# Weight sums of a block product by accumulating DMA, vector sums off GpSimd, prompt rows transposed in spare columns

## Chip, core and metric

The kernel runs on one NeuronCore of a Trainium2 chip, as one launch of one program. The metric is device time in microseconds (us). The engines go by the profile's names: PE (TensorE, with its weight loads as PEld), DVE (VectorE), ACT (ScalarE), POOL (GpSimd) and SP (SyncE, which mainly issues DMAs). Each works through its own instruction stream in order and waits on semaphores.

## What is computed

One layer for 128 prompt tokens and 512 sample tokens of width 1024: a modulated input `h`, a wide projection `h @ w_in`, a gated long convolution by FFT in one branch, windowed attention with 16 heads of 64 in the other, a merge, an output projection and a layer norm. Cut to what matters:

```python
h = x * (1 + scale) + shift
z = h @ w_in                                   # D_IN = 10240 columns
hy, g_h, qkv, g_a, m = split(z)
hy = short_conv(hy, conv_w, conv_b)            # 3 taps
v_h, x1, x0 = split(hy)
u = v_h * x1
y_h = (irfft(rfft(u, 2L) * rfft(filt, 2L))[:L] + u * d_bias) * x0
y_a = attention(q, k, v)                       # sample: 8 x 16 window + context keys; prompt: full
p_h = (y_h * silu(g_h)) @ w_bh
p_a = (y_a * silu(g_a)) @ w_ba
m_h, m_a = split(sigmoid(m))
out = (m_h * p_h + m_a * p_a) @ w_out
x_new = layer_norm(ALPHA * x + gate * out, ln_g, ln_b)
```

The prompt's keys and values are outputs too (`new_k`, `new_v`).

## The kernel before

Every large matmul is made of three passes over operands split in a high part (rounded to fp32r) and a low part (the rest): high x high, high x low, low x high. `split` (L100) makes them: ACT casts the high part (L101), and DVE or GpSimd subtracts it (L102). `hH` and `hL` are the split input, eight blocks of 128 channels by 640 tokens. Weights lie in DRAM as `wall[i]`, 128 x 1024 tiles, and are loaded into two `raw` buffers by SP.

The work has five stages. The prologue (0 to about 55 us) makes the modulated input. The convolution phase (55 to 366) projects the tiles of `hy` on PE and weaves in FFT products. `conv_tile` (L464) evacuates a projection on ACT and adds the outer taps with two instructions on DVE (L477). `product_in_blocks` (L458) multiplies by `x0` on GpSimd. Meanwhile `token_sums` (L685) makes on GpSimd the sums t1 to t4 of blocks of `h`, split, and stores them in DRAM (`tok_d`). The transition (366 to 403) reloads them as `t`. The attention phase (403 to 777) makes the other projections in 22 pairs of tiles and weaves attention into them; a tail (777 to 965) projects, merges and normalizes.

A pair is a 2 x 2 block product with seven block products instead of eight (`pair_tile`, L1067). Its two weight tiles give blocks a11, a12 (first tile) and a21, a22 (second tile). `prepared` (L1039) makes seven weight blocks `wb{tile}_{j}`: j = 0, 4, 5 are a11, a12, a22; s2 = a11 - a21 (j = 2), s1 = s2 - a22 (1) and s6 = a12 + s1 (6) are sums on DVE, s3 = a21 + a22 (3) is one on GpSimd (L1049). Each is split: the low parts of j = 0, 4, 5 are GpSimd's, the rest DVE's. Five `wb` buffers go round. `prepared` is advanced one step per product, so weight blocks come several products ahead, the next pair's first ones during the last products of the pair before.

A head `j` of attend (two heads of 64, L1012) is woven into two or three pairs, counted in half products. `tiled(i)` puts scores of two query blocks in four PSUM banks, does the value products of older blocks, and computes the softmax: a row maximum on DVE (L892), the exponential on ACT (L897), a scaling on GpSimd (L899; L952 for the prompt block `pp`). `turned(i)` transposes the softmax tiles of the two blocks before on PE (L915) into banks `pt` and copies them on ACT (L917) to `pts`. Four banks exist for this (`aux`). For the first block of a head it also transposes the prompt rows `pp` to a bank `ptp` (L1007), copied to `ptsp` (L1009). `pp` and the middle blocks' softmax tiles share one ring of five buffers, `p`; the outer blocks lie in `edge` buffers.

Outside the prologue, a recording layer decides where an instruction stands on its engine, from the order of the code and its own estimate of when inputs are there.

## Time and profile before

| | us |
|---|---|
| median of 3 runs | 969.93 (968.72 to 970.64) |
| the profiled execution's own time | 966.56 |
| its span, first to last instruction | 964.8 |
| mean granted TensorE clock | 0.972 of full |
| busy: PE / DVE / ACT / POOL | 892.5 / 666.8 / 441.2 / 346.2 |
| DMA | 148.76 MB |

In a group's row stand line, engine, operation, output <- inputs by names, shape, and xcount; then busy us and mean ns of one; then the engine's idle time just before such instructions and what ended it. A row of waits reads: who <- what it waited for, us in total, times, longest. A row of the timeline starts with its start in us and its length; a bracket holds the idle time before. A row of windows gives busy us of PE, PEld, DVE, ACT and POOL, the granted clock, the share of the DMA engines and GB/s. Rows of DMA issues end with the median time from issue to landing.

### The profile page before, as it was taken

Reading aid. Unit: us, or ns where it says so; the run is one execution under the profiler, and the core shown is the slowest. Engines: PE = TensorE matmul, PEld = TensorE weight load, DVE = VectorE, ACT = ScalarE, POOL = GpSimd, SP = SyncE. Lnnn points to the kernel's source line nnn. Section 1 sums busy time; section 2 is a strip of 40 time slices with the busy share of each in tenths; the row PEclk is TensorE's granted clock in tenths of the full one; section 3 lists DMA queues with packets and bytes.
Section 4 is the critical chain, followed back from the end, with each engine's and each line's share of the span. In section 5 each row is a group of like instructions: output and inputs, shape, how many; then the busy total and the mean of one; then the engine's idle time right before and its main releaser. Section 6 shows DMA issues by size and latency. Waiting matters only on the chain. (4 is left out here: it accounts for less than half of the span.)

```text
span 964.8 us, 17002 instructions
## 1 busy us (share of the span) xinstructions
PE 892.5 (93%) x6464; PEld 850.8 (88%) x6464; DVE 666.8 (69%) x1179; ACT 441.2 (46%) x950; POOL 346.2 (36%) x330
## 2 busy tenths in 40 slices
PE   8799999799999997798988989999898999999994
PEld 7699999799999996698988989888888889999883
DVE  4887766984794786577676857677676558577565
ACT  4276445444644524454555546555556532143200
POOL 0740115542210304584764666556746500000000
PEclk9999999899999998899999999999999999999997
DMA  8966675567564514743534252613433377535331
GB/s 333 365 182 140 139 175 133 149 162 175 136 133 126 138 55 175 277 149 98 166 97 150 75 165 93 193 59 113 138 109 107 107 251 270 208 137 201 120 106 66
DMA packets 61998, 148.76 MB, mean 154 GB/s; under 512 B 9531, under 2 KB 27195, under 8 KB 61916
## 3 DMA queue, kind: packets, MB, share of 16 engines
q1 hardware_dynamic: 49580, 116.90, 36.7%
q0 software_dynamic: 6720, 25.17, 11.9%
q10 hardware_dynamic: 5616, 5.61, 1.7%
q8 instruction: 51, 0.84, 0.3%
q14 instruction: 31, 0.25, 0.1%
HBM read 123.66 MB, written 23.99 MB: 153 GB/s over the span
## 5 line engine op out<-in xcount | busy, mean ns | idle before, releaser
L1080 PE MATMUL sp<-t,wb 128*128 128x320 f32 x1056 | 180.4, 323 | 22.6 <-POOL wb L102 11.4
L1080 PEld LDWEIGHTS sp<-t,wb 128*128 128x128 f32 x1056 | 164.6, 196 | 30.0 <-POOL wb L102 13.3
L1080 PE MATMUL sp<-hH,wb 128*128 128x320 f32 x528 | 128.1, 314 | 0.0
L102 POOL TENSOR_TENSOR wb<-raw,wb 128x512 fp32r<-128x512 f32 x66 | 89.5, 1360 | 87.9 <-ACT wb L101 79.6
L170 PE MATMUL mm<-hH,wh 128*128 128x320 f32 x416 | 100.5, 315 | 4.2 <-ACT hH L316 4.0
L170 PE MATMUL mm<-hH,wl 128*128 128x320 f32 x416 | 99.9, 312 | 0.4 <-DVE wl L102 0.4
L170 PE MATMUL mm<-hL,wh 128*128 128x320 f32 x416 | 99.7, 312 | 0.3 <-DVE hL L317 0.3
L1080 PEld LDWEIGHTS sp<-hH,wb 128*128 128x128 f32 x528 | 91.1, 189 | 3.3 <-issue 2.5
L150 POOL DMA_DIRECT2D wl<-wall x28 | 25.0, 891 | 164.1 <-ACT wl L149 142.7
L101 ACT ACTIVATE wb<-s 128x512 fp32r<-128x512 f32 x88 | 54.7, 627 | 62.7 <-DVE s L1049 40.0
L1080 PE MATMUL sp<-hL,wb 128*128 128x320 f32 x264 | 81.8, 310 | 0.0
L102 DVE TENSOR_TENSOR wb<-s,wb 128x512 fp32r<-128x512 f32 x88 | 71.1, 819 | 14.4 <-ACT wb L101 14.1
L170 PEld LDWEIGHTS mm<-hH,wh 128*128 128x128 f32 x416 | 70.8, 190 | 6.0 <-ACT hH L316 4.5
L170 PEld LDWEIGHTS mm<-hL,wh 128*128 128x128 f32 x416 | 71.1, 190 | 1.5 <-DVE hL L317 1.1
L170 PEld LDWEIGHTS mm<-hH,wl 128*128 128x128 f32 x416 | 71.1, 190 | 1.5 <-DVE wl L102 0.9
L1359 POOL TENSOR_TENSOR r<-r,bc 128x64 f32<-128x64 f32 x1 | 0.3, 320 | 182.2 <-ACT r L1358 182.2
L899 POOL TENSOR_SCALAR p<-p,sm 128x384 f32<-128x384 f32 x32 | 46.6, 1462 | 34.2 <-DVE sm L898 34.1
L101 ACT ACTIVATE wb<-raw 128x512 fp32r<-128x512 f32 x66 | 41.1, 623 | 34.7 <-DMA raw<-wall 24.6
L151 ACT ACTIVATE wh<-raw 128x1024 fp32r<-128x1024 f32 x28 | 29.7, 1059 | 52.7 <-PE mm L170 37.5
L1080 PEld LDWEIGHTS sp<-hL,wb 128*128 128x128 f32 x264 | 50.0, 189 | 0.0
L1049 DVE TENSOR_TENSOR s<-raw,raw 128x512 f32<-128x512 f32 x22 | 16.8, 762 | 43.3 <-DMA raw<-wall 42.4
L101 ACT ACTIVATE wh<-raw 128x1024 fp32r<-128x1024 f32 x21 | 22.1, 1059 | 52.3 <-PE mm L170 41.5
(356 smaller groups left out, 2291.5 us busy)
## 6 DMA issues: line engine op xcount, KB each, us to landing
raw<-wall SPq DMA_DIRECT2D x96, 512.0 KB, 3.7
wl<-wall POOLq DMA_DIRECT2D x28, 512.0 KB, 6.1
ada<-wada SPq DMA_DIRECT2D x16, 512.0 KB, 8.2
tm<-bias SPq DMA_DIRECT2D x16, 512.0 KB, 5.0
tok_d<-t POOLq DMA_DIRECT2D x16, 320.0 KB, 5.2
t<-tok_d SPq DMA_DIRECT2D x16, 320.0 KB, 5.6
gate<-wgate SPq DMA_DIRECT2D x8, 512.0 KB, 5.0
wo<-wall SPq DMA_DIRECT2D x8, 512.0 KB, 3.9
```

The costliest lines, as they stand in the source:

```text
L101: hi = nc.scalar.activation(dst_h, src, AF.Copy)
L102: return hi, (eng or nc.vector).tensor_tensor(dst_l, src, f(dst_h), op=ALU.subtract)
L150: nc.gpsimd.dma_start(wl, a["wall"][i], accum_op=ALU.add)
L151: nc.scalar.activation(wh, raw[:], AF.Copy)
L170: nc.tensor.matmul(ps[hf][:, :HALF], wt[k], x[:, hf * HALF : (hf + 1) * HALF], start=(i == 0 and k == 0), stop=(i == lead[2] and k == NK - ...
L899: nc.gpsimd.tensor_scalar_mul(pv, pv, sm[:, 2:3])
L1049: (nc.gpsimd if j in ON_POOL["sums"] else nc.vector).tensor_tensor(src[j], x, y, op=op)
L1080: nc.tensor.matmul(dst, wk, x(xi, k), start=j < 4 and k == 0 and i == 0, stop=k == 3 and i == 2, skip_group_check=True,)
L1359: nc.gpsimd.tensor_tensor(r[:, h], r[:, h], bc[:, 0, h], op=ALU.mult)
```

## The change

GpSimd is left with scalings, memsets, a last small sum and DMA issues. (1) Token sums and products with `x0` go to DVE, the high parts of the token sums to ACT, and the product in `gates_h` to DVE. (2) In `prepared` the second tile counts with its sign turned, so s2 = a11 + a21 and s3 = a21 + a22 need only additions of weights. s3 is made in place by a DMA from DRAM that adds onto a21 in the raw tile; s2 is loaded a second time from DRAM and gets a21 by such a DMA. Both are issued by GpSimd. s1 = s2 + a22 and s6 = a12 + s1 stay on DVE, and all seven low parts are DVE's. Where the second tile's result is used its sign is turned back by a scale or a constant. (3) All keys of the prompt are copied once on ACT before they are stored. (4) The prompt rows are transposed together with the third block (b = 2) of their head into columns 384 to 511 of its banks, and copied with it; the copies have 512 columns and four buffers.

```diff
     def product_in_blocks(y, x, u):
-        nc.gpsimd.tensor_tensor(y[:, :LP], x[:, :LP], u[:, :LP], op=ALU.mult)
+        nc.vector.tensor_tensor(y[:, :LP], x[:, :LP], u[:, :LP], op=ALU.mult)
...
-    def gate(th, p):
-        nc.vector.scalar_tensor_tensor(th, th, 1.0, p[:, :HALF], op0=ALU.add, op1=ALU.mult)
+    def gate(th, p, one=1.0):
+        nc.vector.scalar_tensor_tensor(th, th, one, p[:, :HALF], op0=ALU.add, op1=ALU.mult)
...
-        def step(dst, x, i, j, op):
+        def step(dst, i, j, op):
             for t in (hH, hL):
-                nc.gpsimd.tensor_tensor(dst, x, part(t, i, j), op=op)
-                x = dst
+                nc.vector.tensor_tensor(dst, dst, part(t, i, j), op=op)
...
-            nc.gpsimd.tensor_copy(two(hi), t)
-            nc.gpsimd.tensor_tensor(two(lo), t, f(two(hi)), op=ALU.subtract)
+            split(two(hi), two(lo), t)
...
-        nc.gpsimd.tensor_tensor(a_, part(hH, 0, 1), part(hL, 0, 1), op=ALU.add)
-        yield
-        step(b_, a_, 0, 0, ALU.subtract)
+        nc.vector.tensor_tensor(a_, part(hH, 0, 1), part(hL, 0, 1), op=ALU.add)
+        yield
+        nc.vector.tensor_tensor(b_, part(hH, 0, 0), a_, op=ALU.subtract)
+        nc.vector.tensor_tensor(b_, b_, part(hL, 0, 0), op=ALU.add)
...
-    def k_half(j, hf, src, psum=True):
+    def k_half(j, hf, src, sign=1.0):
...
-            nc.scalar.activation(shape(k[:, cs]), x, AF.Copy)
+            nc.scalar.activation(shape(k[:, cs]), x, AF.Copy, scale=sign)
         if not hf:
-            kp = src[:, PS_]
-            if psum:
-                kp = const.tile([P, P], F32, tag="kp", name=f"kp{j}")[:]
-                nc.scalar.activation(kp, src[:, PS_], AF.Copy)
+            kp = const.tile([P, P], F32, tag="kp", name=f"kp{j}")[:]
+            nc.scalar.activation(kp, src[:, PS_], AF.Copy, scale=sign)
...
-            nc.vector.tensor_tensor(shape(kl[:, cs]), x, f(shape(k[:, cs])), op=ALU.subtract)
+            nc.vector.scalar_tensor_tensor(shape(kl[:, cs]), x, sign, f(shape(k[:, cs])), op0=ALU.mult, op1=ALU.subtract)
...
-    def transposed(j, b, ps):
+    def transposed(j, b, ps, pp=None):
         res = []
         for h in range(2):
             pt = aux(f"pt{j}_{h}_{b}")
             for i, (_, c) in enumerate(CHUNKS[b]):
                 nc.tensor.transpose(pt[:, i * P : i * P + P], ps[h][:, c : c + P], ident)
-            ptS = at.tile([P, 384], F32, tag="pts", bufs=5, name=f"pts{j}_{h}_{b}")
-            nc.scalar.activation(ptS[:], pt[:, :384], AF.Copy)
+            n = 384
+            if pp is not None:
+                nc.tensor.transpose(pt[:, 384:], pp[:, h], ident)
+                n = 512
+            ptS = at.tile([P, 512], F32, tag="pts", bufs=4, name=f"pts{j}_{h}_{b}")
+            nc.scalar.activation(ptS[:, :n], pt[:, :n], AF.Copy)
...
-            pvm(o_[rows(h)], val(j, 0, h), head[j]["ptp"][:, h * P : h * P + P], True, True)
+            pvm(o_[rows(h)], val(j, 0, h), head[j]["t", 2][h][:, 384:], True, True)
...
-            if b == 0:
-                pt = aux(f"ptp{j}")
-                for h in range(2):
-                    nc.tensor.transpose(pt[:, h * P : h * P + P], st_["pp"][:, h], ident)
-                ptp = st_["ptp"] = at.tile([P, 2 * P], F32, tag="pts", bufs=5, name=f"ptsp{j}")
-                nc.scalar.activation(ptp[:], pt[:, : 2 * P], AF.Copy)
-            st_["t", b] = transposed(j, b, st_[b])
+            st_["t", b] = transposed(j, b, st_[b], st_["pp"] if b == 2 else None)
...
-    ON_POOL = dict(sums=(3,), lows=(0, 4, 5))
-    blocks, made = [], {}
+    SIGN = (1.0, -1.0)
+    made = {}
...
     def prepared(i0, i1):
+        wall = a["wall"]
         for i in (i0, i1):
-            if i not in raws:
-                wraw(i)
+            wraw(i)
         ra, rb = raws.pop(i0), raws.pop(i1)
-        a11, a12, a21, a22 = (r[:, 512 * h : 512 * h + 512] for r in (ra, rb) for h in range(2))
-        src = {0: a11, 4: a12, 5: a22}
-
-        def wsum(j, x, y, op, dst=None):
-            src[j] = dst if dst is not None else sp.tile([P, 512], F32, tag="s", bufs=2, name=f"s{j}_{i0}")[:]
-            (nc.gpsimd if j in ON_POOL["sums"] else nc.vector).tensor_tensor(src[j], x, y, op=op)
-
-        wsum(2, a11, a21, ALU.subtract)
-        wsum(1, src[2], a22, ALU.subtract)
+        a11, a12, s3, a22 = (r[:, 512 * h : 512 * h + 512] for r in (ra, rb) for h in range(2))
+        nc.gpsimd.dma_start(s3, wall[i1][:, 512:], accum_op=ALU.add)
+        s1, s2 = (sp.tile([P, 512], F32, tag="s", bufs=2, name=f"s{j}_{i0}")[:] for j in (1, 2))
+        load_to(s2, wall[i0][:, :512])
+        nc.gpsimd.dma_start(s2, wall[i1][:, :512], accum_op=ALU.add)
+        src = {0: a11, 1: s1, 2: s2, 3: s3, 4: a12, 5: a22, 6: s1}
         for j in range(7):
-            if j == 3:
-                wsum(3, a21, a22, ALU.add)
-                wsum(6, a12, src[1], ALU.add, src[1])
+            if j == 1:
+                nc.vector.tensor_tensor(s1, s2, a22, op=ALU.add)
+            elif j == 3:
+                nc.vector.tensor_tensor(s1, a12, s1, op=ALU.add)
             n = len(made)
             w = made[i0, j] = wp.tile([P, 2, 512], F32R, tag=RING[n % 5], bufs=2 if RING[n % 5] == "wh" else 3, name=f"wb{i0}_{j}")
-            split(w[:, 0], w[:, 1], src[j], nc.gpsimd if j in ON_POOL["lows"] else None)
+            split(w[:, 0], w[:, 1], src[j])
...
             elif j == 1:
-                nc.vector.tensor_tensor(u, dst, u, op=ALU.add)
+                nc.vector.tensor_tensor(u, u, dst, op=ALU.subtract)
...
-            gate(sg, src)
+            gate(sg, src, SIGN[i])
...
-            nc.scalar.activation(th, src, AF.Tanh, scale=0.5)
+            nc.scalar.activation(th, src, AF.Tanh, scale=0.5 * SIGN[i])
...
-            gate(th, src)
-            nc.gpsimd.tensor_tensor(th, th, yu[i, hf], op=ALU.mult)
+            gate(th, src, SIGN[i])
+            nc.vector.tensor_tensor(th, th, yu[i, hf], op=ALU.mult)
```

How the change moves instructions, at the three places on which steps of the prediction rest. A row is an instruction with its line, output, inputs and tile; the brackets name the engines and DMA queues whose semaphores it waits for (DMAHW: issued by SP or ACT, DMASW: issued by POOL); `wb70_1` is weight block 1 of the pair that starts with tile 70.

First, ACT at the second turn of head 3 (the turn for blocks 2 and 3, `pts3_..`), while the pair 37 is multiplied and the pair 70 is prepared. Before:

```order
L101 ACTIVATE wb37_5_6797<-raw45_6616 128x512 [waits DMAHW1_49]
L897 ACTIVATE p4_1_1_6779,sm4_1_1_6780<-p4_1_1_6779,sm4_1_1_6780 128x384 [waits DVE_49]
L101 ACTIVATE wb37_6_6814<-s1_37_6620 128x512 [waits PE_49,Activation_49]
L101 ACTIVATE wb70_0_6840<-raw70_6832 128x512 [waits DMAHW6_49,PE_49]
L808 ACTIVATE k5_6857<-c2_37_6830 128x64 [waits DVE_49]
L808 ACTIVATE k5_6857<-c2_37_6830 128x2x128
L786 ACTIVATE q5_6878<-sp37_0_6705 128x128 [waits PE_49]
L786 ACTIVATE q5_6878<-sp37_0_6705 128x128
L786 ACTIVATE q5_6878<-sp37_0_6705 128x64
L917 ACTIVATE pts3_0_2_6899<-pt3_0_2_6895 128x384 [waits PE_49]
L917 ACTIVATE pts3_1_2_6905<-pt3_1_2_6901 128x384 [waits PE_49]
L917 ACTIVATE pts3_0_3_6911<-pt3_0_3_6907 128x384 [waits PE_49]
```

After:

```order
L1080 ACTIVATE u37_6787<-sp37_0_6697 128x320 [waits PE_49]
L101 ACTIVATE wb37_5_6789<-raw45_6608 128x512
L101 ACTIVATE wb37_6_6806<-s1_37_6611 128x512 [waits PE_49]
L101 ACTIVATE wb70_0_6833<-raw70_6824 128x512 [waits DMAHW3_49,PE_49]
L101 ACTIVATE wb70_1_6857<-s1_70_6829 128x512 [waits DVE_49,PE_49]
L807 ACTIVATE k5_6850<-c2_37_6822 128x64 [waits DVE_49]
L807 ACTIVATE k5_6850<-c2_37_6822 128x2x128
L785 ACTIVATE q5_6872<-sp37_0_6697 128x128 [waits PE_49]
L785 ACTIVATE q5_6872<-sp37_0_6697 128x128
L785 ACTIVATE q5_6872<-sp37_0_6697 128x64
L101 ACTIVATE wb70_2_6880<-s2_70_6830 128x512 [waits DMASW0_49]
L918 ACTIVATE pts3_0_2_6894<-pt3_0_2_6889 128x512 [waits PE_49]
```

The casts of weight blocks 1 and 2 of pair 70 stood behind the four copies; now they stand ahead of the first one, and block 2's waits for an accumulating DMA (DMASW). The fourth exponential of head 4's first tiles (`p4_1_1`) went the other way: it stood well ahead of the copies and now comes behind them.

Second, PE at the same turn: the transposes of head 3's blocks 2 and 3, between the products of pair 37. Before:

```order
L915 MATMUL pt3_0_2_6895<-pack2_378,p3_0_2_6446 128x128 x3
L915 MATMUL pt3_1_2_6901<-pack2_378,p3_1_2_6452 128x128 x3
L915 MATMUL pt3_0_3_6907<-pack2_378,edge30_4210 128x128 [waits PE_49]
L915 MATMUL pt3_0_3_6907<-pack2_378,edge30_4210 128x128 x2
L915 MATMUL pt3_1_3_6913<-pack2_378,edge31_4212 128x128 [waits PE_49]
L915 MATMUL pt3_1_3_6913<-pack2_378,edge31_4212 128x128 x2
```

After:

```order
L912 MATMUL pt3_0_2_6889<-pack2_378,p3_0_2_6445 128x128 [waits Pool_49]
L912 MATMUL pt3_0_2_6889<-pack2_378,p3_0_2_6445 128x128 x2
L915 MATMUL pt3_0_2_6889<-pack2_378,pp3_6099 128x128
L912 MATMUL pt3_1_2_6896<-pack2_378,p3_1_2_6451 128x128 [waits Pool_49]
L912 MATMUL pt3_1_2_6896<-pack2_378,p3_1_2_6451 128x128 x2
L915 MATMUL pt3_1_2_6896<-pack2_378,pp3_6099 128x128
L912 MATMUL pt3_0_3_6903<-pack2_378,edge30_4210 128x128 [waits PE_49,Pool_49]
L912 MATMUL pt3_0_3_6903<-pack2_378,edge30_4210 128x128 x2
L912 MATMUL pt3_1_3_6909<-pack2_378,edge31_4212 128x128 [waits Activation_49,Pool_49]
L912 MATMUL pt3_1_3_6909<-pack2_378,edge31_4212 128x128 x2
```

Two transposes of the prompt rows (L915) came in, and the last bank, `pt3_1_3`, is now one for which PE waits for ACT (it held `pt3_0_2`), where before it waited for nothing but PE itself.

Third, PE in the convolution phase, at the forward transform of the second group's channels (`c1_X1`, `s1_X1`), between products (`mm13`, `mm18`, `mm19`) of the projection. Before:

```order
L170 MATMUL mm18_1_2228<-hH_85,wh18_2222 128x320
L170 MATMUL mm18_0_2227<-hL_86,wh18_2222 128x320
L170 MATMUL mm18_1_2228<-hL_86,wh18_2222 128x320
L170 MATMUL mm18_0_2227<-hH_85,wl18_2223 128x320
L158 MATMUL c1_X1_1874<-uh1_2_1851,dftH_99 128x256 [waits Activation_49]
L158 MATMUL s1_X1_1875<-uh1_2_1851,dftH_99 128x256 [waits PE_49]
L170 MATMUL mm18_1_2228<-hH_85,wl18_2223 128x320
L170 MATMUL mm18_0_2227<-hH_85,wh18_2222 128x320
L159 MATMUL c1_X1_1874<-ul1_2_1852,dftH_99 128x256 [waits DVE_49]
L160 MATMUL c1_X1_1874<-uh1_2_1851,dftL_100 128x256
```

After:

```order
L170 MATMUL mm19_0_2365<-hL_86,wh19_2360 128x320
L170 MATMUL mm19_1_2366<-hL_86,wh19_2360 128x320
L170 MATMUL mm19_0_2365<-hH_85,wl19_2361 128x320
L170 MATMUL mm19_1_2366<-hH_85,wl19_2361 128x320
L170 MATMUL mm19_0_2365<-hH_85,wh19_2360 128x320
L170 MATMUL mm19_1_2366<-hH_85,wh19_2360 128x320
L170 MATMUL mm19_0_2365<-hL_86,wh19_2360 128x320
L170 MATMUL mm19_1_2366<-hL_86,wh19_2360 128x320
L170 MATMUL mm19_0_2365<-hH_85,wl19_2361 128x320
L159 MATMUL c1_X1_1874<-ul1_2_1852,dftH_99 128x256 [waits DVE_49]
L160 MATMUL c1_X1_1874<-uh1_2_1851,dftL_100 128x256
```

Before, the product that waits for DVE's low part `ul1_2` stands in the first third of tile 18's matmuls; now all of tile 18 stands ahead of it, and it comes within tile 19.

More of the change, by code (lines that the diff above doesn't have):

```diff
@@ L709, in token_sums @@
         yield
-        nc.gpsimd.tensor_tensor(a_, part(hH, 1, 1), a_, op=ALU.subtract)
-        nc.gpsimd.tensor_tensor(a_, a_, part(hL, 1, 1), op=ALU.add)
+        nc.vector.tensor_tensor(a_, part(hH, 1, 1), a_, op=ALU.subtract)
+        nc.vector.tensor_tensor(a_, a_, part(hL, 1, 1), op=ALU.add)
         yield
@@ L714, in token_sums @@
         yield
-        step(b_, b_, 1, 1, ALU.subtract)
+        step(b_, 1, 1, ALU.add)
         yield
@@ L718, in token_sums @@
         yield
-        step(b_, b_, 1, 0, ALU.add)
+        step(b_, 1, 0, ALU.subtract)
         yield
```

4 lines of the change are left out of this document (2 added, 2 removed).

## Prediction

> **What bounds the kernel now.** I read the page's first part, then busy time by stage, then what TensorE (PE) waited for. The first view says which engine is full.
>
> ```profile
> span 964.8 us, 17002 instructions
> PE 892.5 (93%) x6464; PEld 850.8 (88%) x6464; DVE 666.8 (69%) x1179; ACT 441.2 (46%) x950; POOL 346.2 (36%) x330
> ```
>
> PE is busy 93% of the span, so the change can give at most PE's idle time and what a reduced clock costs it. The stages, and one slice of 25 us (columns: length, busy PE, weight loads, DVE, ACT, POOL, granted clock, DMA share, GB/s):
>
> ```profile
> 0.00:55.00 55.00, 47.18 (x477) 40.14 (x478) 38.05 (x60) 22.17 (x38) 18.60 (x25) 0.97 0.80 306
> 55.00:366.00 311.00, 301.15 (x2190) 298.35 (x2189) 228.53 (x294) 156.15 (x307) 83.96 (x91) 0.99 0.58 143
> 375.00:775.00 400.00, 362.01 (x2691) 341.17 (x2690) 273.53 (x636) 213.85 (x541) 242.17 (x211) 0.96 0.42 138
> 500.00:525.00 25.00, 21.91 (x161) 21.11 (x162) 13.75 (x37) 12.78 (x30) 11.53 (x10) 0.93 0.62 193
> ```
>
> PE idles 7.8 us in the prologue, 9.9 us in the convolution phase, and 38.0 us in the attention phase, where POOL is at its busiest (242 of 400 us) and the clock at its lowest. What PE waited for, from the view of waits:
>
> ```profile
> PE pt L915 <- ACT ptsp L1009: 13.1, 7, 3.5
> PE sp L1080 <- POOL wb L102: 11.4, 7, 5.7
> PE sp L1080 <- DVE wb L102: 6.3, 8, 2.5
> PE c_X L159 <- DVE ul L102: 6.2, 1, 6.2
> ```
>
> The first three are what the change edits directly; the fourth hangs on GpSimd in another way, shown next.
>
> **Convolution phase: sums leave GpSimd.** DVE's short convolution (L477) has two inputs in SBUF, and its mean differs between tiles:
>
> ```profile
> L477 DVE SCALAR_TENSOR_TENSOR x<-zs,pack,x 128x641 f32<-128x641 f32 x32 | 34.3, 1071 | 2.5 <-ACT x L475 2.1
> L477 DVE SCALAR_TENSOR_TENSOR u<-zs,pack,u 128x641 f32<-128x641 f32 x16 | 25.1, 1572 | 4.9 <-ACT u L475 4.8
> ...
> 173.42 11.62 DVE L477 SCALAR_TENSOR_TENSOR u<-zs,pack,u 128x641 f32<-128x641 f32 x2 [0.87 <-ACT u L475]
> 176.80 1.87 POOL L700 TENSOR_TENSOR t<-ts,t 128x640 fp32r<-128x640 f32 x1
> ...
> 185.42 0.58 PE L159 MATMUL c_X<-ul,dftH 128*128 128x256 f32 x1 [6.17 <-DVE ul L102]
> 185.62 0.87 DVE L477 SCALAR_TENSOR_TENSOR x<-zs,pack,x 128x641 f32<-128x641 f32 x1
> ...
> 187.00:189.00 2.00, 2.00 (x11) 2.00 (x10) 1.68 (x3) 0.38 (x1) 0.00 (x0) 0.50 0.00 0
> ```
>
> Two such instructions took 11.62 us while POOL ran its token sums, of which the first is shown, and 0.87 us each with POOL quiet. PE stood 6.17 us for it and was then still at half clock (0.50) at 189, which from 185.4 on costs another 1.8 us. At 0.87 us all 48 would take 41.8 instead of 59.4 us, so 17.6 us of DVE come free. Against that the change gives DVE 26 token sums and 24 product pieces. A DVE sum of that size is priced by
>
> ```profile
> L500 DVE TENSOR_TENSOR u<-u,x 128x641 f32<-128x641 f32 x8 | 6.6, 826 | 0.1
> ```
>
> that is 26 x 0.83 = 21 us, and 8 tiles of products of 640 columns at about 0.9 us are 7 us. DVE's load therefore rises by some 11 us, part of it in the prologue: at most 240 of 311 us, no bound. The 6.17 + 1.8 us go, since the changed program also puts matmuls of another projection on PE ahead of the product that waits (shown with the change): **-8**. In the prologue I set DVE's relief and its added sums equal: 0, bounds -3 and +3. For this stage: -12 to +4.
>
> **Transition (366 to 403): about nothing.** DMA sets this stage:
>
> ```profile
> 375.00:400.00 25.00, 16.72 (x78) 13.65 (x77) 13.38 (x33) 10.10 (x28) 14.82 (x21) 0.66 1.02 386
> 387.97 0.60 PE L1080 MATMUL sp<-t,wb 128*128 128x320 f32 x1 [5.67 <-POOL wb L102]
> ```
>
> The 5.67 us are put down to POOL, but with a DMA share of 1.02 I choose to read it as the token operand `t` landing late; taking POOL away does not bring that earlier. One part weight (256 KB, 0.7 us at 386 GB/s) now loads ahead of it and one 512 KB load (1.4 us) behind it: **-1**, bounds -4 and +5.
>
> **Attention: prompt rows.** The old form needs a fifth PSUM bank in the odd turns, and PE waits for a copy (L1009) that stands in ACT's queue behind weight casts:
>
> ```profile
> 517.45 0.36 ACT L1009 ACTIVATE ptsp<-ptp 128x256 f32<-128x256 f32 x1
> ...
> 517.86 0.90 PE L915 MATMUL pt<-pack,p 128*128 128x128 f32 x3 [2.68 <-ACT ptsp L1009]
> ```
>
> Without that bank the wait goes, except in head 0's first turn, where the after program still reuses two banks (1.1 us): **-12** of 13.1. The wider copies (512 for 384 columns, 16 of them) cost ACT about 0.1 us each, the removed ones 0.37 us: nothing. The 25 us slice with this wait (500 to 525, quoted with the stages) has a clock of 0.93, 1.75 us short of full; the view of windows has four such slices in the phase, and I take two halves of that, 1.75 us, as regained: **-2**.
>
> **Attention: weight parts.** Removed, moved and added, per instruction:
>
> ```profile
> L102 POOL TENSOR_TENSOR wb<-raw,wb 128x512 fp32r<-128x512 f32 x66 | 89.5, 1360 | 87.9 <-ACT wb L101 79.6 <-issue 6.5 <-DMA yh_d<-th 1.4
> L1049 POOL TENSOR_TENSOR s<-raw 128x512 f32<-128x512 f32 x22 | 32.2, 1464 | 36.5 <-DVE wb L102 36.5
> L1137 POOL TENSOR_TENSOR th<-th,yur 128x320 f32<-128x320 f32 x16 | 16.0, 1003 | 7.4 <-DVE th L482 7.3
> L150 POOL DMA_DIRECT2D wl<-wall x28 | 25.0, 891 | 164.1 <-ACT wl L149 142.7 <-PE ut L528 11.2 <-PE fa L160 7.6
> L102 DVE TENSOR_TENSOR wb<-s,wb x88: 672/691/1814, 376.8 to 767.5; 128x512 fp32r<-128x512 f32 x88
> L1049 DVE TENSOR_TENSOR s<-raw,raw 128x512 f32<-128x512 f32 x22 | 16.8, 762 | 43.3 <-DMA raw<-wall 42.4
> ```
>
> POOL loses 89.5 + 32.2 + 16.0 us and gains 44 accumulate issues of 0.89 us (39 us, from L150). DVE gains 66 lows of 0.69 (45.5 us) and 16 gate products, two thirds of a low's columns, 0.48 (7.7 us); it loses 22 sums (16.8 us), and I take 15 us of disturbance off (88 lows at 819 ns mean against the median of 691 give 11.3 of it). So 273.5 + 45.5 + 7.7 - 16.8 - 15 = 295 of about 380 us: no bound on average. A low right behind its cast on DVE ends 0.6 us sooner than on POOL, and no longer waits for scalings. Of POOL's 11.4 us, 5.67 belong to the transition; the other **-5.7** go. Of DVE's 6.3 us I let **-2.3** go, since DVE is less disturbed but fuller.
>
> The accumulates themselves are not in this part of the trace. The nearest row is
>
> ```profile
> wl<-wall POOLq DMA_DIRECT2D x28, 512.0 KB, 6.1
> raw<-wall SPq DMA_DIRECT2D x96, 512.0 KB, 3.7
> ```
>
> 256 KB thus land in 3.1 us (by bytes) to 6.1 us (if it is all fixed); I take 4.5. The 22 pairs fill the 400 us, 18 us each, and a weight part is needed about seven products, one pair, after the step that frees its raw tile. Load 3.7 + accumulate 6.1 + sum, cast and low 2.0 = 11.8 us at worst: covered by 6 us. Traffic grows by 0.75 MB a pair, 16.5 MB over 380 us: 43 GB/s on 138, and share 0.42 becomes about 0.56. Cost nothing; if the cover were gone, see the slower rival. The signs (scale -1, `one` = -1) ride in operands that exist: nothing.
>
> **Attention: a new wait.** The prompt block now stays in the five-buffer ring `p` until the second turn of its head, so the fourth softmax tile of the next head (L889) waits for PE's transposes of the old one, keeps its PSUM bank meanwhile, and PE's fourth transpose group there needs the bank of the first, hence ACT's first copy. In heads 0 to 5, six turns, that copy stands behind the next pair's casts 0, 1 and 2 (the order listing). Rows of before at such a turn:
>
> ```profile
> 536.56 0.62 ACT L101 ACTIVATE wb<-raw 128x512 fp32r<-128x512 f32 x1
> 540.13 1.28 POOL L102 TENSOR_TENSOR wb<-raw,wb 128x512 fp32r<-128x512 f32 x1
> 541.46 0.86 PE L1080 MATMUL sp<-t,wb 128*128 128x320 f32 x4 [0.57 <-POOL wb L102]
> 542.15 0.82 PE L915 MATMUL pt<-pack,p 128*128 128x128 f32 x6
> 542.68 1.64 ACT L917 ACTIVATE pts<-pt 128x384 f32<-128x384 f32 x4 [1.49 <-PE pt L915]
> 544.86 0.69 DVE L1049 TENSOR_TENSOR s<-raw,raw 128x512 f32<-128x512 f32 x1 [2.50 <-DMA raw<-wall]
> ```
>
> The low that frees the raw tile ends at 541.4 on POOL; on DVE it can end at 537.9, 0.7 us behind its cast. The load took 3.45 us to the sum's start (541.41 to 544.86): 541.4. Then sum 0.69, cast 0.62, the k and q casts 1.1, cast 0.61 and the copy 0.5: 544.9. PE has three groups transposed by about 543.2 (542.15 - 0.57 + 9 of 12 transposes at 0.14 + its products): it waits some 1.7 us. Six times, less one in six for turns where DVE's earlier softmax shortens it: **+9**, bounds 0 and +22 (3.6 each, with the accumulate at 6.1).
>
> **The sum** is -8 - 1 - 12 - 2 - 5.7 - 2.3 + 9 = -22. The profiled execution took 966.56 us (span 964.8); 944.6 after. The median of the three runs shown is 969.93, 3.4 us above it, so I forecast **948 us**; own range 938 to 957.
>
> **Rivals.**
> - *The new wait takes most of it back.* For: the copy's queue has three casts, one behind a load, an accumulate and a sum. Against: POOL's late low goes. At +22 instead of +9 the sum is -9: 961 us. Chance 0.15.
> - *Everything goes.* All 38 us of the attention phase cannot, but -12 there by weights, +2 for the new wait, and -12 in the convolution phase give -36: 934 us; down to 926 if the clock stays whole. For: the waits on POOL are all short of DVE's free time. Chance 0.2.
> - *DVE becomes the bound.* POOL still scales the softmax tiles (32 x 1.46 + 32 x 1.16 + 16 x 0.64 = 94 us), and DVE's maximum low is 1.81 us. If each scaling holds DVE for its length, 295 + 94 = 389 us of DVE work stand in 400, with waits in its queue: the attention phase stays at 395 to 400 and only the convolution gain is left, 958 to 968 us. The Trainium skill has such a rule (SBUF — State Buffer, "Who interferes with whom"): a DVE instruction with two SBUF inputs contends with a GpSimd instruction that reads SBUF, by an exclusive lock; it agrees with the 11.62 us above and speaks against a full relief here, where 154 lows instead of 88 meet the scalings. Against: the median low is 691 ns beside a POOL that is busy 60%. Chance 0.1, a part of it no change.
> - *Slower: accumulates come late.* They share POOL's in-order queue with scalings that wait for DVE, and DVE's s1 waits for the accumulate, with softmax and lows behind it. It decides once a landing slips more than the 6 us of cover above; at 7.5 us late each of 22 pairs loses 1.5 us: +33 on -22, 981 us. For: POOL's queue is in order, and a scaling at its head holds what follows. Against: the cover, and a half empty DMA. Chance 0.13.
> - *Transfers were the matter all along*, so the edits only shift which engine is named: the weight waits stay, 966 to 972 us. Chance 0.05.
>
> **How the numbers follow.** Forecast 0.37, then the chances above. About 0.2% (2 us) is what a measurement of this kernel can tell from no change. Range 927 to 970: it leaves out the slower rival and what lies below 927. Faster: 0.37 + 0.15 + 0.2 + 0.08 of DVE as the bound = 0.80; within 0.2%: its other 0.02 and 0.04 of the last rival, 0.06; slower: 0.13 and the last 0.01, 0.14.
>
> **What would show it.** The lows and sums of POOL gone; L477 near 0.87 us; no wait at c_X; no wait on L1009's kind in the odd turns, and in six even turns `pt` waiting for ACT `pts` by 1 to 2 us; accumulates landing in 3 to 6 us. I am wrong if `pt` waits exceed 4 us each, if `sp` waits for DVE `wb` by more than 10 us in all, if DVE waits for the accumulates of `s` or `raw`, or if the DMA share passes 0.8 in the attention phase.

## The result

| | before | after |
|---|---|---|
| median, same set of runs | 969.33 (967.78 to 970.64) | 955.33 (953.14 to 959.01) |
| ratio after/before | | 0.986 [0.9825, 0.9895] |
| span of the profiled execution | 964.8 | 951.0 |

The change is 14 us faster; 948 was forecast. The head of the page of after, and its row of the stage of attention (columns as with the stages of before):

```profile
span 951.0 us, 17183 instructions
PE 887.0 (93%) x6464; PEld 851.5 (90%) x6464; DVE 654.0 (69%) x1289; ACT 445.5 (47%) x956; POOL 179.9 (19%) x212
...
375.00:775.00 400.00, 368.57 (x2746) 354.93 (x2747) 272.33 (x691) 215.79 (x534) 136.17 (x137) 0.95 0.63 177
```

POOL loses half of its work, DVE does not grow, and the granted clock of the attention phase is 0.95, where 0.96 stood before. What PE waits for in after:

```profile
PE pt L912 <- ACT pts L918: 22.2, 8, 3.3
PE sp L1073 <- ACT wb L101: 9.4, 1, 9.4
PE sp L1073 <- DMA t<-tok_d: 4.6, 2, 2.5
PE sp L1073 <- DVE c L1088: 2.7, 3, 2.0
```

Every wait that the prediction named at the start is gone: `ptsp`, the lows of `wb` on POOL and on DVE, and `c_X`. In their place stand one that was foreseen, at twice its size (22.2 us), and one of 9.4 us that was not.

Since both programs do the same matmuls, the time can be split at three places that both have (ahead of, between and behind them the numbers of matmuls agree to within three): the last product of a value tile `v` with `wh` (the end of the convolution phase), the first product of probabilities and values (head 0's), and the last product of a weight part. They are read from the first and last starts in the views of the tiles `v`, `pts` and `wb`; before:

```profile
L644 PE MATMUL v<-wh,hH x128: 276/281/365, 120.2 to 350.0; 128*128 128x256 f32 x128
L922 PE MATMUL s<-pts,v x224: 272/273/324, 424.2 to 751.4; 128*64 128x128 f32 x112
L1080 PE MATMUL sp<-hH,wb x528: 305/310/633, 366.7 to 777.0; 128*128 128x320 f32 x176
```

and the same three views of after:

```profile
L644 PE MATMUL v<-wh,hH x128: 276/281/365, 116.6 to 338.3; 128*128 128x256 f32 x128
L923 PE MATMUL s<-pts,v x252: 272/273/324, 418.6 to 742.2; 128*64 128x128 f32 x126
L1073 PE MATMUL sp<-hH,wb x528: 305/310/616, 354.9 to 765.5; 128*128 128x320 f32 x176
```

| stage (us) | before | after | difference | forecast |
|---|---|---|---|---|
| start to end of convolution phase | 350.0 | 338.3 | -11.7 | -8 |
| transition and head 0 | 74.2 | 80.3 | **+6.1** | -1 |
| the other heads | 352.8 | 346.9 | **-5.9** | -13 |
| rest | 187.8 | 185.5 | -2.3 | 0 |

The forecasts of the third row are all the terms from the prompt rows to the new wait (-12, -2, -5.7, -2.3, +9). The convolution phase gave more than was promised; the transition with head 0 and the other heads together owe 14 us. The -2.3 in the rest is not read: the kernels below have 185 to 190 there with code that does not differ in that stage.

**The convolution phase** went as reasoned. Groups of instructions of after, line L477:

```profile
L477 DVE SCALAR_TENSOR_TENSOR x<-zs,pack,x 128x641 f32<-128x641 f32 x32 | 28.2, 883 | 1.7 <-ACT x L475 1.3
L477 DVE SCALAR_TENSOR_TENSOR u<-zs,pack,u 128x641 f32<-128x641 f32 x16 | 14.1, 882 | 4.8 <-ACT u L475 4.6
```

The means were 1071 and 1572 ns with POOL at work. With POOL's sums gone both are 0.88 us. The Trainium skill (SBUF — State Buffer, "Who interferes with whom") states that a DVE instruction with two SBUF inputs contends with a GpSimd instruction that reads SBUF, by an exclusive lock; these means agree with it.

**The new wait**, at one of six like turns, rows picked from the timeline of after:

```profile
479.13 0.33 SPq L63 DMA_DIRECT2D raw<-wall  x1
...
482.48 0.49 PE L912 MATMUL pt<-pack,edge 128*128 128x128 f32 x3
482.69 0.69 DVE L1047 TENSOR_TENSOR s<-s,raw 128x512 f32<-128x512 f32 x1 [1.53 <-DMA raw<-wall]
483.48 0.63 ACT L101 ACTIVATE wb<-s 128x512 fp32r<-128x512 f32 x1 [4.06 <-DVE s L1047]
484.01 0.55 ACT L807 ACTIVATE k<-c 128x64 fp32r<-128x64 f32 x2
484.46 0.54 ACT L785 ACTIVATE q<-sp 128x128 fp32r<-128x128 f32 x3
484.88 0.64 ACT L101 ACTIVATE wb<-s 128x512 fp32r<-128x512 f32 x1
485.40 1.85 ACT L918 ACTIVATE pts<-pt 128x512 f32<-128x512 f32 x4
...
486.15 0.52 PE L912 MATMUL pt<-pack,edge 128*128 128x128 f32 x3 [3.18 <-ACT pts L918]
```

PE has three transpose groups done at 482.97. ACT stood 4.06 us at a cast that waits for the sum `s`. The sum waits for the plain load of the pair's second raw tile, issued at 479.13 and there 3.56 us later, and behind the cast come two copies of `k`, three of `q` and one more cast before the copy that PE needs. The six turns cost 3.33, 3.18, 3.29, 2.77, 3.29 and 3.11 us, 19.0 together, where 1.7 each was forecast. Of the other two of the eight waits, 1.64 us stand in head 0's first turn, foreseen at 1.1, and 1.61 at 735.6, not foreseen.

**The transition.** Rows picked from the timelines of after, POOL, DVE and PE:

```profile
367.82 0.86 POOL L1043 DMA_DIRECT2D s<-wall  x1 [1.17 <-DMA s<-wall]
375.02 0.69 DVE L1047 TENSOR_TENSOR s<-s,raw 128x512 f32<-128x512 f32 x1 [3.35 <-DMA s<-wall]
376.43 8.03 PE L1073 MATMUL sp<-t,wb 128*128 128x320 f32 x36 [9.40 <-ACT wb L101]
```

The first pair's accumulate is issued at 367.8, while the token tiles load; the sum that needs it starts at 375.0, the cast of that sum follows, and PE stands 9.4 us for it. All accumulates of the program, and the token tiles beside them, from the table of DMA issues (their median time to landing last):

```profile
raw<-wall POOLq DMA_DIRECT2D x22, 256.0 KB, 4.1
s<-wall SPq DMA_DIRECT2D x22, 256.0 KB, 2.8
s<-wall POOLq DMA_DIRECT2D x22, 256.0 KB, 4.8
t<-tok_d SPq DMA_DIRECT2D x16, 320.0 KB, 7.4
```

At 4.1 and 4.8 us the accumulates land about as guessed (4.5). So it is not their length that was wrong, if they are at fault at all. Yet one of the signs by which the prediction said it would be wrong is there, DVE waiting for an accumulate:

```profile
DVE s L1047 <- DMA s<-wall: 10.5, 7, 3.4
```

Its other three signs are not: no wait for `pt` is above 3.33 us, `sp` does not wait for DVE's `wb`, and the DMA share is 0.63. What the accumulates cost is what the runs had to tell.

### The profile page after: what moved, and what is told of

Its sections match the earlier page's. It is cut to its first block, busy times and chain, and to the rows that moved or that the text cites. A ratio compares the mean times of both kernels' runs of the same rounds, so it can differ in the third digit from the quotient of the medians.

```text
span 951.0 us, 17183 instructions
## 1 busy us (share of the span) xinstructions
PE 887.0 (93%) x6464; PEld 851.5 (90%) x6464; DVE 654.0 (69%) x1289; ACT 445.5 (47%) x956; POOL 179.9 (19%) x212
## 5 line engine op out<-in xcount | busy, mean ns | idle before, releaser
L1073 PE MATMUL sp<-t,wb 128*128 128x320 f32 x1056 | 172.5, 317 | 14.3 <-ACT wb L101 9.4
L1073 PE MATMUL sp<-hH,wb 128*128 128x320 f32 x528 | 134.4, 327 | 2.5 <-DVE c L1088 2.5
L170 PE MATMUL mm<-hH,wh 128*128 128x320 f32 x416 | 104.7, 314 | 4.4 <-ACT zs L472 2.3
L1073 PEld LDWEIGHTS sp<-hH,wb 128*128 128x128 f32 x528 | 97.2, 201 | 5.9 <-issue 5.4
L102 DVE TENSOR_TENSOR wb<-raw,wb 128x512 fp32r<-128x512 f32 x88 | 63.9, 726 | 43.1 <-ACT wb L101 42.8
L101 ACT ACTIVATE wb<-raw 128x512 fp32r<-128x512 f32 x88 | 54.6, 625 | 55.0 <-DMA raw<-wall 32.6
L101 ACT ACTIVATE wb<-s 128x512 fp32r<-128x512 f32 x66 | 41.0, 627 | 64.9 <-DVE s L1047 48.2
L102 DVE TENSOR_TENSOR wb<-s,wb 128x512 fp32r<-128x512 f32 x66 | 45.9, 698 | 12.8 <-ACT wb L101 12.6
L1322 PE MATMUL out<-woh,yhs 128*128 128x512 f32 (+1 forms) x176 | 45.7, 373 | 0.0
L896 POOL TENSOR_SCALAR edge<-edge,sm 128x320 f32<-128x320 f32 x32 | 39.8, 1252 | 11.8 <-DVE sm L895 11.3
```

Source lines behind the costliest of these rows:

```text
L101: hi = nc.scalar.activation(dst_h, src, AF.Copy)
L102: return hi, (eng or nc.vector).tensor_tensor(dst_l, src, f(dst_h), op=ALU.subtract)
L170: nc.tensor.matmul(ps[hf][:, :HALF], wt[k], x[:, hf * HALF : (hf + 1) * HALF], start=(i == 0 and k == 0), stop=(i == lead[2] and k == NK - ...
L896: nc.gpsimd.tensor_scalar_mul(pv, pv, sm[:, 2:3])
L1073: nc.tensor.matmul(dst, wk, x(xi, k), start=j < 4 and k == 0 and i == 0, stop=k == 3 and i == 2, skip_group_check=True,)
L1322: ins = nc.tensor.matmul(dst, m[k][:, c0 : c0 + P], w[:, c : c + n], start=(first and k == 0), stop=(last and k == 5), skip_group_check=True,)
```

## Experiments

Three questions: does the prompt block in the ring cost what its wait shows; do accumulates that land on time cost anything; and where does the gain come from? Twelve runs were made in three sets (f1 is the kernel of e1 again). Times are medians, with the ratio to the kernel before in the same set (968.13, 969.4 and 968.91 us) and its 95% interval. An interval is 0.2 to 0.3% to either side, so a difference of two kernels below is known to some 2 to 4 us. Stage times use the same three places.

### First set

**e1: the prompt block out of the ring.** After, with `pp` in two buffers of its own; the ring `p` keeps four, and the copies `pts` get two and two.

```diff
-  p = edges[b, h] if b in (0, 3) else at.tile([P, 384], F32, tag="p", bufs=5, ...)
+  p = edges[b, h] if b in (0, 3) else at.tile([P, 384], F32, tag="p", bufs=4, ...)
-  ptS = at.tile([P, 512], F32, tag="pts", bufs=4, ...)
+  ptS = at.tile([P, 512 - 128 * (b % 2)], F32, tag=f"pts{b % 2}", bufs=2, ...)
-  pp = st_["pp"] = at.tile([P, 2, P], F32, tag="p", bufs=5, ...)
+  pp = st_["pp"] = at.tile([P, 2, P], F32, tag="pp", bufs=2, ...)
```

> The changed kernel, but with two buffers of their own for the prompt blocks pp and four for the ring p, so that no softmax tile waits for the turn of the old head. The weight casts still stand ahead of the copies on ACT. Theory (the reused ring buffer holds a PSUM bank, and PE waits for the first copy): the waits of the transposes for ACT's copies fall from 22.2 us to under 4, and the time falls by 15 to 20 us, to about 938. Rival (weight blocks come late by the accumulates, and the copies only show it): PE then waits for weight blocks instead, and the time falls by less than 6 us, to 950 or more.

945.26 us, 0.9774 [0.9744, 0.9804]; run again as f1 in the second set, 943.24, 0.973 [0.9713, 0.9747]. The same kernel thus differs by 0.4% between sets, and smaller differences across sets are not read. PE's waits for `pts` fall from 22.2 to 1.9 us, but only 10 to 12 us come back (8 to 13 by the ratios), between the theory's 15 to 20 and the rival's 6. PE's waits in e1:

```profile
PE sp L1073 <- DVE c L1088: 9.5, 8, 2.6
PE sp L1073 <- ACT wb L101: 9.4, 1, 9.4
```

The mechanism is the predicted one; half of its waiting was cover for others in DVE's queue, on the pair's sum `c` (2.7 to 9.5 us) and on the gates `th` (3.3 us, not among the waits of after).

**e2: the old form of the prompt rows.** After, with the `ptp` bank and its copy of before.

```diff
-  nc.tensor.transpose(pt[:, 384:], pp[:, h], ident)
+  if b == 0:
+      pt = aux(f"ptp{j}")
+      for h in range(2):
+          nc.tensor.transpose(pt[:, h * P : h * P + P], st_["pp"][:, h], ident)
+      ptp = st_["ptp"] = at.tile([P, 2 * P], F32, tag="pts", bufs=5, ...)
+      nc.scalar.activation(ptp[:], pt[:, : 2 * P], AF.Copy)
```

> The changed kernel with the old treatment of the prompt rows (a bank ptp of their own in the odd turns, copied by ACT alone). Theory: the even turns lose their 19 us of waits, the odd turns get back waits for ptsp of 8 to 14 us; the time is 945 to 952, a little better than the changed kernel's 955. Rival (the moved prompt rows gave the gain of the attention phase): 962 to 968.

953.06 us, 0.9847 [0.9822, 0.9873], a little above what was expected and level with after (0.986): 14.4 us of `ptsp` waits stand in place of 22.2 us of `pts` waits. As it was made, the prompt-row edit is worth nothing.

**e3: only the sums of the convolution phase.** Before, with the token sums and the products with `x0` on DVE, and the high parts of the token sums on ACT (two of the lines).

```diff
-  nc.gpsimd.tensor_tensor(y[:, :LP], x[:, :LP], u[:, :LP], op=ALU.mult)
+  nc.vector.tensor_tensor(y[:, :LP], x[:, :LP], u[:, :LP], op=ALU.mult)
...
-  nc.gpsimd.tensor_tensor(a_, part(hH, 0, 1), part(hL, 0, 1), op=ALU.add)
+  nc.vector.tensor_tensor(a_, part(hH, 0, 1), part(hL, 0, 1), op=ALU.add)
```

> The kernel before with only the token sums and the products with x0 moved from GpSimd to DVE (high parts to ACT). Theory: the convolution phase alone gives 9 to 12 us, the last projection ahead of the transition starts at about 341 instead of 352.5, and the attention phase stays as before: 957 to 960. Rival (part of the 11.7 us there is owed to other edits): a gain of under 6 us, 963 or more.

958.38 us, 0.9906 [0.9876, 0.9937]. The convolution phase ends at 337.9 instead of 350.0, and L477's mean is 884 ns: this part alone gives what the whole change gives in that stage (12.1 us against 11.7). Its attention phase still waits as before did, on POOL's lows (4.9), DVE's (6.8) and `ptsp` (11.7).

**e4: the first pair without its `s2` accumulate.** e1, with that one sum on DVE.

```diff
+  if i0 == pairs[0][0]:
+      nc.vector.tensor_tensor(s2, a11, s3, op=ALU.add)
   nc.gpsimd.dma_start(s3, wall[i1][:, 512:], accum_op=ALU.add)
-  load_to(s2, wall[i0][:, :512])
-  nc.gpsimd.dma_start(s2, wall[i1][:, :512], accum_op=ALU.add)
+  if i0 != pairs[0][0]:
+      load_to(s2, wall[i0][:, :512])
+      nc.gpsimd.dma_start(s2, wall[i1][:, :512], accum_op=ALU.add)
```

> As the first run of this set, and for the first pair alone s2 is a sum on DVE, without its second load and its accumulate. Theory (in the transition the first pair's accumulate, behind eleven token loads, lands late): the wait of 9.4 us for the cast of weight block 1 becomes 4 to 6 us for a token load, and the time is 3 to 5 us below the first run. Rival (the token loads set that stage anyway): within 2 us of the first run.

946.44 us, 0.9773 [0.9747, 0.9799], level with e1, which is what the rival said. The wait of 9.4 us is gone, but in PE's waits of e4 stands

```profile
PE sp L1076 <- DMA t<-tok_d: 12.0, 4, 5.1
```

PE now waits for token tiles instead: the 9.4 us were no price of that accumulate alone. Head 0's first product of values comes at 415.8, 78.2 us after the convolution phase (79.3 in e1).

### Second set

All edits stand on e1's kernel, run again as **f1**.

> The first experiment's kernel again (prompt blocks in buffers of their own), on the same chip as the next three, to compare with them: 943 to 947.

**f2: block 0's low on POOL again** and **f3: those of blocks 0, 4 and 5**, as before had them.

```diff
-  split(w[:, 0], w[:, 1], src[j])
+  split(w[:, 0], w[:, 1], src[j], nc.gpsimd if j == 0 else None)           # f2
+  split(w[:, 0], w[:, 1], src[j], nc.gpsimd if j in (0, 4, 5) else None)   # f3
```

> As f1, with the low part of weight block 0 back on GpSimd. In the profile of the first experiment DVE's pair sums (c, L1088) stand behind low 0, which waits for ACT's cast, which waits for the raw tile's load; PE waits 9.5 us in all for those sums and 3.3 us for gates. Theory (moving low 0 to DVE put the pair sums behind a load): these waits fall below 5 us and the time falls by 4 to 8 us against f1. Rival (ACT's queue, where the copies and gates stand behind the same cast, holds them as well): within 2 us of f1.

> As f1, with the lows of blocks 0, 4 and 5 back on GpSimd, as in the kernel before, and only the sums left to the DMA. Theory: POOL's slow lows behind the scalings bring back 4 to 8 us of waits for weight blocks, and DVE's are a little fewer: f1 -2 to +6 us. Rival (the move of the lows is what gave the gain in the weights): f1 +8 us or more.

f2: 953.89 us, 0.9848 [0.9819, 0.9877], 10.7 slower than f1. The theory (relief for the sum `c` behind that low) was wrong, and so was the rival (no difference), though PE's waits for `c` fall from 10.8 to 7.4 us. f3: 965.55 us, 0.996 [0.9937, 0.9982], 22.3 slower than f1, the rival's result; nearly all that f1 had gained on before is gone. Among PE's waits in f3 is

```profile
PE sp L1073 <- POOL wb L102: 9.7, 9, 2.4
```

and, as ACT's longest wait there,

```profile
ACT wb L101 <- DMA raw<-wall: 58.4, 22, 5.4
```

against 39.1 us in f1 and 47.4 in f2. A low on POOL takes 1.40 us (91.7 us for 66 in f3) against 0.7 on DVE. As these waits are read here, it frees the raw tile later, the next load starts later, and the next pair's cast waits. With accumulates in the program, moving the 66 lows to DVE is worth 22 us.

**f4: the two sums on DVE.** f1 without accumulating DMAs and without the second load of `s2`.

```diff
-  nc.gpsimd.dma_start(s3, wall[i1][:, 512:], accum_op=ALU.add)
-  load_to(s2, wall[i0][:, :512])
-  nc.gpsimd.dma_start(s2, wall[i1][:, :512], accum_op=ALU.add)
+  nc.vector.tensor_tensor(s2, a11, s3, op=ALU.add)
+  nc.vector.tensor_tensor(s3, s3, a22, op=ALU.add)
```

> As f1, with s2 and s3 as sums on DVE: no accumulating DMA in the pairs, no second load, 16.5 MB less traffic. It tests whether the accumulates are hidden. Theory (they are, and DVE has the time for 44 more sums of 0.69 us, 30 us on 270 of 385, but not without some delay): f1 -2 to +6 us. Rival 1 (the accumulates and their traffic delay the raw loads): 4 us or more below f1. Rival 2 (DVE is the bound): f1 +10 us or more.

**929.47 us** (928.42 to 932.34), 0.9592 [0.9575, 0.961]: 13.8 us below f1, the first rival's result. DVE has 44 sums more and the program is faster. The attention phase of f1, by its row in the view of windows,

```profile
375.00:775.00 400.00, 374.63 (x2805) 359.48 (x2806) 272.32 (x700) 216.94 (x537) 134.35 (x137) 0.97 0.65 186
```

and of f4:

```profile
375.00:775.00 400.00, 383.71 (x2885) 369.81 (x2886) 303.35 (x750) 218.59 (x538) 96.72 (x95) 0.97 0.46 151
```

PE does 9 us more work in the same 400 us, with DVE at 303 (no bound), POOL at 97, and a DMA share of 0.46 instead of 0.65. So the accumulates, with the second load of `s2` that they need, were costed at nothing and cost 13.8 us. Where, is seen in f1's timeline, rows picked (SP, ACT, DVE, PE), through one pair:

```profile
505.19 1.60 SPq L63 DMA_DIRECT2D raw<-wall  x2
511.73 0.63 ACT L101 ACTIVATE wb<-raw 128x512 fp32r<-128x512 f32 x1 [3.97 <-DMA raw<-wall]
512.39 0.69 DVE L102 TENSOR_TENSOR wb<-raw,wb 128x512 fp32r<-128x512 f32 x1 [4.55 <-ACT wb L101]
513.63 0.38 PE L1073 MATMUL sp<-hH,wb 128*128 128x320 f32 x1 [2.37 <-DVE c L1088]
518.14 1.15 ACT L101 ACTIVATE wb<-raw 128x512 fp32r<-128x512 f32 x2 [1.15 <-DMA raw<-wall]
519.82 0.68 DVE L102 TENSOR_TENSOR wb<-raw,wb 128x512 fp32r<-128x512 f32 x1
520.53 0.33 SPq L63 DMA_DIRECT2D raw<-wall  x1
```

The raw tiles run in a closed loop: load, casts, last low (here of the first tile, 519.82, 0.68 long), and 0.03 us after that low's end SP issues the next load (520.53). At the first cast of the pair that was loaded from 505.19 on, ACT stands 3.97 us; DVE's low and the sum `c` stand behind the cast, and PE waits 2.37 us. The accumulate into `s3` (which lies in the raw tile) adds a second wait of ACT inside the loop, at 518.14.

### Third set

**g3: only `s3` by accumulate.** f1, with `s2` summed on DVE.

```diff
-  load_to(s2, wall[i0][:, :512])
-  nc.gpsimd.dma_start(s2, wall[i1][:, :512], accum_op=ALU.add)
+  nc.vector.tensor_tensor(s2, a11, s3, op=ALU.add)
```

> As f1 (prompt blocks in buffers of their own, 943 us), with s2 as a sum on DVE and s3 still by an accumulating DMA. Theory A (s2's load and accumulate stand ahead of block 1's sum, s3's have a product's time more): 930 to 935, near f4. Rival (s3's accumulate in place, which needs the raw tile and lets it go late, costs as much): 936 to 941.

940.75 us, 0.9689 [0.967, 0.9709]: 11 us above f4 and 2.5 below f1 (9 and 4 by the ratios), where the second is within what sets differ by. That is the rival's result: most of the price is that of the accumulate into the raw tile. Pair by pair, g3's timeline (POOL, ACT):

```profile
507.29 0.63 ACT L101 ACTIVATE wb<-raw 128x512 fp32r<-128x512 f32 x1 [1.71 <-DMA raw<-wall]
510.04 0.90 POOL L1042 DMA_DIRECT2D raw<-wall  x1 [5.82 <-DVE s L1041]
514.24 0.63 ACT L101 ACTIVATE wb<-raw 128x512 fp32r<-128x512 f32 x1 [1.60 <-DMA raw<-wall]
```

and f4's (ACT), for the same two casts, of blocks 0 and 3:

```profile
506.73 0.63 ACT L101 ACTIVATE wb<-raw 128x512 fp32r<-128x512 f32 x1 [1.94 <-DMA raw<-wall]
512.46 0.62 ACT L101 ACTIVATE wb<-raw 128x512 fp32r<-128x512 f32 x1
```

From cast 0 to cast 3 it is 6.95 us in g3 and 5.73 in f4, 1.22 more in this pair. Over the program ACT's casts wait 41.8 us for `raw` in 24 places in g3, 39.1 in 21 in f1, and 25.3 in 13 in f4.

**g2: the sums on DVE, the prompt block still in the ring.** After with f4's edit.

> The changed kernel with s2 and s3 as sums on DVE, and with the prompt blocks still in the ring p: the order of PE and ACT around the second turns is as in the changed kernel, without the accumulates. Theory (the wait there is ring and bank, lengthened by the accumulates in ACT's queue): the waits of the transposes for ACT's copies are 10 to 16 us instead of 22, and the time is 935 to 943. Rival (the whole wait came by the accumulates): under 4 us of such waits, within 3 us of f4. Other rival (the accumulates have no part in it): 20 us or more of such waits.

937.76 us, 0.9673 [0.9644, 0.9703]. PE's wait for `pts` in g2:

```profile
PE pt L912 <- ACT pts L918: 12.8, 8, 3.0
```

The same six turns now cost 3.02, 2.09, 1.77, 1.24, 2.10 and 1.79 us: 2.0 in the mean, where the prediction had 1.7 and after has 3.2. Against f4 the ring costs 8.3 us.

The timelines show how the accumulates lengthen these waits. From the issue of the second raw tile's load to PE's fourth transpose group it is 7.5 us in the mean of the six turns, in after and in g2 alike (the load itself is 0.4 us longer in after, the way from the sum to PE 0.3 us shorter). But PE has its third group done 4.3 us after that issue in after and 5.5 in g2: with accumulates the load goes out 1.2 us later, as PE sees it. Which instructions of the pair ahead hold the load back was not followed one by one.

**g4: the old prompt rows with the sums on DVE** (the edit of e2 on g2's kernel, so that `pp` lies in the ring `p` as in before).

> As f4, with the old treatment of the prompt rows (bank ptp). It prices the prompt rows where nothing else hides them: theory, 6 to 14 us of waits for ptsp come back and the time is 936 to 944; rival, these waits came from casts that are now earlier: within 3 us of f4.

938.35 us, 0.9679 [0.9653, 0.9705], with `ptsp` waits of 13.8 us again. Against f4, turning the prompt rows in spare columns is thus worth 8.9 us, together with the buffers of its own that `pp` then needs, and with the sums on DVE.

**g1: traffic alone.** f4 with three unread DRAM copies of 256 KB for each pair, to tell the transfers' weight from their place in the queues.

```diff
+  n = [p[0] for p in pairs].index(i0)
+  nc.sync.dma_start(spare_d[3 * n], wall[i0][:, :512])
+  for d in range(2):
+      nc.gpsimd.dma_start(spare_d[3 * n + 1 + d], wall[i1][:, 512 * d : 512 * d + 512])
```

> As f4 (all sums on DVE, 929.5 us), with three DMAs of 256 KB a pair added from the weights to DRAM scratch that nobody reads, one issued by SP and two by POOL, at the place where the accumulates were: the traffic of the accumulates without any work that waits for them. Theory A (it is the latency: block 1's sum, and with it ACT's and DVE's queues, wait for a load and an accumulate in a row): within 4 us of f4. Theory B (it is the traffic, which delays the raw tiles' loads): 8 to 14 us over f4.

978.58 us, 1.0093 [1.0064, 1.0121], and no answer. Nothing orders copies that read an input and are read by no one, and all 66 were issued in the first 65 us; PE's longest wait in g1 is

```profile
PE adaT L241 <- DMA ada<-wada: 38.1, 4, 28.9
```

The convolution phase ends 48.4 us later than in f4 (386.5 against 338.1), and from there to the last weight part it is 403.6 us against 404.3. How much of the accumulates' price is the share of the DMA engines, and how much their latency in ACT's queue, this run does not tell. The traces of the others tell a part. The plain loads of raw tiles between 400 and 740 us, from the tables of DMA issues of f4, g3 and f1 in that order (median time to landing last):

```profile
raw<-wall SPq DMA_DIRECT2D x42, 512.0 KB, 4.0
raw<-wall SPq DMA_DIRECT2D x42, 512.0 KB, 4.1
raw<-wall SPq DMA_DIRECT2D x40, 512.0 KB, 4.6
```

With one accumulate a pair and no second load (g3, share 0.54) these loads are 0.1 us slower than in f4, at most 4 us over 42 of them, and most of the price is there already. That speaks for latency in g3. With all the transfers (f1, share 0.65) the loads take 0.6 us longer, so there the transfers hold each other up as well. How the price divides between the two stays open.

## Why the prediction was right, and where its sizes were wrong

The sign held, and so did the mechanism of most terms. The size was 8 us off (-14 for -22), because of one term above all.

- **The failed term: "Cost nothing" for the accumulates.** They cost 13.8 us with `pp` in its own buffers (f1 against f4), 17.6 with it in the ring (after, 955.33, against g2, 937.76). The prediction set 11.8 us of load, accumulate, sum, cast and low against 18 us a pair, and called the rest cover. The landing time was right (4.1 and 4.8 us for 4.5). What was wrong is the 18 us as the measure: the raw tile does not have a pair's time to spare, since its next load starts 0.03 us after a low has freed it, and ACT stands at such a load's cast already. A wait added inside that loop comes back in every pair, though not in full (13.8 us over 22 is 0.63 us each; in g3 11 us or 0.5 each, for 1.22 in the pair shown). The price is measured; that the loop makes it is read from the traces, and slower loads may have a part in it.
- **The new wait (+9)** was named rightly, with its turns and its queue. Its waits are 19.0 us where 10 were worked out; its price is 8.3 us with the sums on DVE (g2 against f4) and 10 to 12 with accumulates (e1 and f1 against after). The bound of +22 allowed for it. From the low that frees the tile the prediction counted 7.0 us to ACT's copy and 5.3 to PE's third group. The first was nearly right (7.5 to PE's fourth group), and the second came to 4.3 in after and 5.5 in g2: the accumulates send the load out later, where the prediction's upper bound had put an accumulate behind it.
- **Prompt rows (-12)** measure -8.9 with `pp` in its own buffers (g4 against f4), and the wait went as said. Together with the ring, the edit is worth nothing (e2 against after, g4 against g2, both within what sets differ by), where the prediction's two terms left -3.
- **Weights (-5.7 and -2.3)** were too small: 22.3 us for the lows (f3 against f1, both with accumulates). The sum counted only the waits that PE itself shows. That a low on DVE ends sooner than on POOL it noted, but gave no value to the raw tile, and so the next load, coming earlier.
- **Convolution phase (-8)** measured -11.7, within its bounds, and -12.1 in e3. The views above divide it. At the first product of `v`, with 926 matmuls done in both, after is already 3.6 us ahead (116.6 against 120.2), where the prediction set its prologue at 0. The other 8.1 us come behind it, where the wait at `c_X` was, as forecast.
- **Transition (-1, bounds -4 and +5)** measured +6.1, outside. Without any accumulate it is +2.7 (f4: 338.1 to 415.0, or 76.9 us), with that of `s3` alone +2.1 (g3: 338.8 to 415.1), with both +4.9 (f1: 338.3 to 417.4): the load and accumulate of `s2` cost this stage some 3 us, though out of the first pair alone they give back only 1 (e4 against e1). With the edits of the convolution phase alone it is +1.3 (e3: 337.9 to 413.4). The token tiles land later in after (7.4 us, 5.6 before, 5.3 in f4), but in g3 too (7.7), so that does not set the length. What makes the rest was not traced.
- **Clock (-2)**: the granted clock shows nothing of it in after (0.95 against 0.96 over the attention phase; f1 and f4 have 0.97). PE's busy time for the matmuls of the other heads did fall, from 325.9 to 323.5 us, so the term stays open.

Of the rivals, *DVE becomes the bound* is refuted by f4, which gives DVE 44 instructions more than after and is the fastest. DVE's busy time over the attention phase was 272 us in after, not the 295 worked out. The rule of the Trainium skill on the lock (SBUF — State Buffer, "Who interferes with whom") was taken to speak against full relief, yet the 154 lows on DVE in after have means of 726 ns (88 of them) and 698 ns (66), below the 819 ns of before. POOL is busy 136 of those 400 us instead of 242, and where it gets lows back (f3, 218 us) the mean of the lows made from `s` rises from 700 ns in f1 to 821. *Slower, because accumulates come late* had the right suspect: DVE and ACT do wait for them, but at 0.6 us a pair, not at the 33 us in all it was priced at. *The new wait takes most of it back* gave 961 for a price of 22 us; by itself it is half of that. *Everything goes* (934) is about where the program stands without accumulates (g2 938, f4 929). *Transfers were the matter all along* (966 to 972) did not come: the waits for weights on POOL and DVE are gone and the time fell.

Read by parts, the measured -14 is a gain of 31.2 us (g2 against 968.91), which the forecast's 22 underestimated by 9, less 17.6 us of a cost that it set at nothing. The two errors partly cancel, and that is luck: the time in the range is less of a success than it looks.

The best version is f4: sums and lows on DVE, no accumulating DMA, `pp` in its own buffers. It takes 929.47 us, 0.9592 [0.9575, 0.961] of before, and 2.7% less than after.

## What to carry to other kernels

Whether a longer transfer is covered is asked of the buffer's loop, not of the period: find what its next load starts on and who already waits for that load, and if there is no gap, a part of each microsecond put between load and last reader is paid each time round (here about 0.5 us a pair). Work taken off a slow engine can pay by when it frees a buffer, more than by the waits that the profile puts under that engine's name (here 22 us, where 8 were counted). Before work leaves a busy engine for a transfer, compare with simply keeping it: a DVE at 303 of 400 us had room for 44 sums that cost 0.69 us each, and the transfers in their place cost more than those.

## What the runs showed of the hardware

- An accumulating transfer of 256 KB into SBUF landed in 4.1 and 4.8 us where the plain load of 256 KB took 2.8; its issue holds POOL for 0.88 to 0.89 us.
- DVE's subtraction of two SBUF inputs (the lows from `s`, 128x512) took 700 ns in the mean with POOL busy 134 of 400 us (f1) and 821 ns with POOL busy 218 (f3).
- Unordered copies of 16.5 MB in all, issued in the first 65 us (g1), moved PE's work by 48 us through loads that stood beside them, though the copies themselves were used by nobody.
